# Retention part of a two-layer decoder trunk: state products first, a PSUM bank for each head, squares summed by ScalarE's accumulator

## The chip, the cores and the metric

The kernel runs on one core of a Trainium2 chip. The metric is the device time of one execution in microseconds (us). The core's engines are named as in the profile: PE (TensorE matmuls), PEld (its weight loads), DVE (VectorE), ACT (ScalarE), POOL (GpSimd) and SP (SyncE, which here only issues loads).

## What is computed

Two layers over 512 tokens of width 1024. Each layer normalises x, projects it, runs three mixers side by side (retention, stick-breaking attention, a state-space model), gates them, projects and adds. The change lies in retention alone:

```
def retention(q, k, v, q_norm, k_norm, out_norm, cos, sin):
    ...
    inner = jnp.einsum('bnhij,bnjhe->bnihe', scores, vc)        # within a chunk of 128 tokens
    ...
    def step(state, kv):
        return state * chunk_decay + kv, state
    _, prev = lax.scan(step, jnp.zeros_like(chunk_kv[0]), chunk_kv)
    cross = jnp.einsum('bnihd,nbhde->bnihe', qc * q_decay[:, :, None], prev)
    out = (inner + cross).reshape(B_, S_, RET_HEADS, RET_V_DIM)
    out = rmsnorm(out, out_norm.reshape(RET_HEADS, RET_V_DIM))  # per head, over 256 columns
```

There are 4 heads with 128 columns of q and k and 256 of v, and 4 chunks of 128 tokens.

## The kernel before, in words

**Main work and slots.** The body of a layer is a list of pieces of projection (`mains`), each 12 or 24 matmuls of 128x512 into a tile `mm`, at one piece for each slot. A full-precision product is made of three fp32r ones (`three`): weight and activation are split into a high and a low part. ScalarE makes the high part of a weight tile (`wh`), VectorE the low one (`wl`); SP loads the raw tile. All else is written as generators: `spawn(gen, slot)` puts one in a slot, `yield n` moves its rest n slots on, and `yield 0` puts its rest behind the matmuls of the same slot (`late`). The order of instructions on each engine is the order in which this program writes them; nothing is reordered afterwards. An engine that waits holds back everything behind it in its own queue.

**Buffers.** PSUM has 8 banks: three for `mm`, five for everything else (`psm`, pool `ps_sm`, a bank for each tile). SBUF work tiles (`bt`) come from one pool of 48. A new tile takes a buffer that an earlier tile gives back, and its first writer waits for the last reader of that one.

**Retention.** `ret_chunk(n)` runs for chunk n = 0..3, three slots apart, when q, k and v of all chunks are there. It makes the scores of 4 heads in one tile `rs` (four fp32 products of 128x128), masks them into `sT`, and then goes through two parts c = 0, 1 of two heads each; below, part (n, c) is part c of chunk n. Between parts lie two slots, so that the parts of neighbouring chunks interleave: (0,0), (0,1), (1,0), (1,1), (2,0), (2,1), (3,0), (3,1). A part splits v (`rvsh`, `rvsl`), scores (`sTs`) and k (`kts`) and has on PE

- the output tile `ro`, 128x512, one bank: for each of its two heads three split products of 128x256 and, for n > 0, one fp32 product of the chunk's q with the running state (two PE instructions in the trace, `ro<-state,rT`);
- for n < 3 the update of the state, `rkv`, one bank, six split products.

After the matmuls of the slot the state is copied (n = 0, L1252) or added up on DVE from `rkv`, ScalarE squares `ro` into `sq2` (L1258), DVE sums the squares of each head (TENSOR_REDUCE, L1260), and POOL makes the factor `rs` = (mean + eps)^-0.5. Two slots later (`K["t3"]`) DVE writes `yt` = `ro` times the factor; this is the last reader of the bank. Later, `rz_evac` transposes `yt` on PE into `yaT`.

Of the five small banks a part holds one for `ro` over these two slots, and one for `rkv` until the state is updated; the next chunk's `rs` holds one until `sT` is made.

Of the kernel before, what the change touches and what calls it, by code (L numbers as in the profile page):

```python
# [13 lines left out]
AF = mybir.ActivationFunctionType  # L14
ALU = mybir.AluOpType
PSUM = bass.MemoryType.PSUM

P = 128
# [168 lines left out]
def trunk(ctx: ExitStack, tc, x_in, w_in, par_in, bc_in, ng_in, cst_in, rope_in, out):  # L187
    nc = tc.nc
    load = {"V": 0.0, "G": 0.0, "T": 0.0}

    def counted(f, engine, each):


        def g(*a, **k):
            o = k["out"] if "out" in k else a[0]
            load[engine] += 0.07 * (engine != "T") + each * math.prod(o.shape[1:])
            return f(*a, **k)  # L197

        return g

    TT = counted(nc.vector.tensor_tensor, "V", 1.04e-3)
    TS = counted(nc.vector.tensor_scalar, "V", 1.04e-3)
    STT = counted(nc.vector.scalar_tensor_tensor, "V", 1.2e-3)
    GT, GS = counted(nc.gpsimd.tensor_tensor, "G", 2.2e-3), counted(nc.gpsimd.tensor_scalar, "G", 1.2e-3)
    ACT = nc.scalar.activation
    MM = counted(nc.tensor.matmul, "T", 0.42e-3)
# [9 lines left out]
    def bt(name, dt=F32, shape=(P, 512)):  # L216
        return bp.tile(list(shape), dt, tag="b", name=name)

    def st(name, n):
        return sp.tile([P, n], F32, tag="s", name=name, padded_shape=[P, 64])  # L220
# [4 lines left out]
    def psm(name):  # L225
        return ps_sm.tile([P, 512], F32, tag="sm", name=name)
# [14 lines left out]
    def C(n):  # L241
        o, s = CST[n]
        return cst[:, o : o + s]
# [7 lines left out]
        out=negm, in_=negm, pattern=[[1, P]], base=0, channel_multiplier=-1, compare_op=ALU.is_ge, fill=0.0  # L251
# [25 lines left out]
    def rsqrt_mean(out_, ssum, n, eps, cols):  # L277

        t = st("ms", cols)
        GS(out=t, in0=ssum, scalar1=1.0 / n, scalar2=eps, op0=ALU.mult, op1=ALU.add)  # L280
        GT(out=out_, in0=t, in1=mhalf[:, :cols], op=ALU.pow)

    def split(src, name, shape=(P, 512)):
        h = bt(name + "h", F32R, shape)
        l = bt(name + "l", F32R, shape)
        ACT(h, src, AF.Copy)
        TT(out=l, in0=src, in1=h.bitcast(F32), op=ALU.subtract)
        return h, l

    def packed(src, name, op=TT):  # L290
        t = bt(name, F32R)
        ACT(t[:, 0:256], src, AF.Copy)
        op(out=t[:, 256:512], in0=src, in1=t[:, 0:256].bitcast(F32), op=ALU.subtract)
        return t
# [45 lines left out]
    def three(ps, a, b, first, last):  # L340

        MM(ps, a[0], b[0], start=first, stop=False)
        MM(ps, a[0], b[1], start=False, stop=False)
        MM(ps, a[1], b[0], start=False, stop=last)
# [321 lines left out]
    def v3(ap, n=32):  # L666
        return ap.rearrange("p (g m) -> p g m", m=n)
# [173 lines left out]
    def layer(l, last, base):  # L841
# [311 lines left out]
        qT, kT, ktok = [], [], [None] * NT  # L1153
        rv = [[None] * 2 for _ in range(NT)]
        ytok = [[None] * 2 for _ in range(NT)]
# [50 lines left out]
        state = [None, None]  # L1206

        def ret_chunk(n):
            pt = psm("rs")
            for h in range(4):  # L1210
                hs = slice(h * P, h * P + P)
                MM(pt[:, hs], kT[n][:, hs], qT[n][:, hs], start=True, stop=True)
            yield 0
            sT = bt("sT")
            TT(out=v3(sT, P), in0=v3(pt, P), in1=C("tri").unsqueeze(1).to_broadcast(r4h), op=ALU.mult)
            keep = n < NT - 1

            def halves(c):

                cs = slice(256 * c, 256 * c + 256)  # L1220
                return (
                    split(rv[n][c], "rvs"), packed(sT[:, cs], "sTs"),
                    packed(ktok[n][:, cs], "kts", GT) if keep else None,
                )

            part = halves(0)
            yield K["t1"]
            for c in range(2):
                vs, sTs, ks = part
                po = psm("ro")  # L1230
                for i in range(2):
                    h = 2 * c + i
                    hs = slice(h * P, h * P + P)
                    sl = slice(256 * i, 256 * i + 256)
                    two = [slice(P * i, P * i + P), slice(256 + P * i, 256 + P * i + P)]
                    v = [x[:, sl] for x in vs]
                    three(po[:, sl], [sTs[:, x] for x in two], v, True, n == 0)
                    if n:
                        MM(po[:, sl], qT[n][:, hs], state[c][:, sl], start=False, stop=True)
                if keep:  # L1240
                    pk = psm("rkv")
                    for i in range(2):
                        h = 2 * c + i
                        sl = slice(256 * i, 256 * i + 256)
                        two = [slice(P * i, P * i + P), slice(256 + P * i, 256 + P * i + P)]
                        three(pk[:, sl], [ks[:, x] for x in two], [x[:, sl] for x in vs], True, True)
                yield 0
                if not keep:
                    pass
                elif n == 0:  # L1250
                    state[c] = bt(f"state{c}")
                    nc.vector.tensor_copy(out=state[c], in_=pk)  # L1252
                else:
                    TT(out=state[c], in0=state[c], in1=pk, op=ALU.add)
                if c == 0:
                    part = halves(1)
                s2 = bt("sq2")
                ACT(s2, po, AF.Square)  # L1258
                ss, rs = st("ss", 2), st("rs", 2)
                nc.vector.tensor_reduce(out=ss, in_=v3(s2, 256), axis=mybir.AxisListType.X, op=ALU.add)  # L1260
                rsqrt_mean(rs, ss, 256, EPS, 2)
                yield K["t3"]
                ytok[n][c] = bt("yt")
                TT(out=v3(ytok[n][c], 256), in0=v3(po, 256), in1=rs.unsqueeze(2).to_broadcast([P, 2, 256]), op=ALU.mult)

        def rz_evac(m, ps):
            pt = psm("yaT")
# [93 lines left out]
        for n in range(NT):  # L1361
            spawn(ret_chunk(n), at["rv1"] + K["ret0"] + K["ret_gap"] * n)
# [14 lines left out]
        for name, m in mains:  # L1377
            i = now[0]
# [22 lines left out]
    while due:  # L1401
        i = min(due)
# [28 lines left out]
```

## Time and profile before

| | |
|---|---|
| device time, median of 3 runs (range) | 1289.89 us (1289.74 to 1291.02) |
| device time of the profiled execution | 1291.43 us |
| its span, first to last instruction | 1289.7 us |
| PE busy | 1271.6 us, 99% |
| PEld, DVE, ACT, POOL busy | 1051.8, 845.1, 536.9, 388.4 us |
| mean granted TensorE clock | 0.996 of full speed |

PE is the engine that is hardly ever idle, so a change shows in the time where it makes PE wait or takes work or a wait from it. The 1.73 us between time and span lie outside the profiled instructions. The time of the profiled execution is 1.54 us above the median.

### The profile page before, as it was taken

How to read it: one execution, taken by the hardware profiler on the slowest of the kernel's cores; microseconds unless marked ns; L12 is line 12 of the kernel's file. 1: busy time of each engine (PE TensorE's matmuls, PEld its weight loads, DVE VectorE, ACT ScalarE, POOL GpSimd, SP SyncE). 2: the span in 40 equal slices, each digit the busy share in tenths (PEclk: the TensorE clock that was granted, in tenths of full speed). 3: DMA queues.
4: the chain of work that ended last, by engine and by line, in shares of the span. 5: the costliest groups of instructions: out<-in, count | busy, mean ns of one | idle time of the engine just before them, and what ended most of it. 6: DMA issues, size and time to landing. Idle time of an engine off the chain costs nothing.

```text
span 1289.7 us, 16710 instructions
## 1 busy us (share of the span) xinstructions
PE 1271.6 (99%) x6388; PEld 1051.8 (82%) x6388; DVE 845.1 (66%) x1192; ACT 536.9 (42%) x919; POOL 388.4 (30%) x453
## 2 busy tenths in 40 slices
PE   8999999999999999999999989999999999999998
PEld 6887788888888888888888877888888888888887
DVE  6988976866784448555374678778657834675542
ACT  5444454454444433332343545534534544433311
POOL 3314743546531012000052136444565311210000
PEclk9999999999999999999999989999999999999999
DMA  5323222124223322234442312122231232222342
GB/s 211 101 96 98 67 66 82 66 82 131 66 66 99 98 75 72 84 97 155 147 166 72 98 49 66 49 83 82 96 101 66 70 127 82 66 82 83 97 137 75
DMA packets 37235, 119.53 MB, mean 93 GB/s; under 512 B 4130, under 2 KB 4770, under 8 KB 37156
## 3 DMA queue, kind: packets, MB, share of 16 engines
q1 hardware_dynamic: 29376, 104.87, 25.1%
q10 hardware_dynamic: 7780, 13.60, 3.1%
q8 instruction: 50, 0.82, 0.3%
q14 instruction: 29, 0.24, 0.1%
HBM read 114.26 MB, written 4.19 MB: 92 GB/s over the span
## 4 chain that ended last, share of the span: by engine, by line
PE 82%; DVE 3%; ACT 1%; issue 0%; DVEq 0%; ACTq 0%
PE mm L197 71%; PE T L411 2%; PE ro L197 2%; PE py L197 1%; DVE kp L1083 1%; PE S L197 1%; PE sbo L197 1%; PE wt L1100 1%; DVE w L197 1%; PE z L197 1%; PE rkv L197 1%; PE rs L197 1%; PE yaT L1269 1%; DVE ks L197 0%; DVE ybl L197 0%; PE pk L197 0%
## 5 line engine op out<-in xcount | busy, mean ns | idle before, releaser
L197 DVE TENSOR_TENSOR wl<-raw,wh 128x1024 fp32r<-128x1024 f32 x196 | 249.6, 1280 | 100.8 <-ACT wh L320 97.1
L197 PE MATMUL mm<-hh,wh 128*128 128x512 f32 x640 | 256.2, 400 | 0.0
L197 PE MATMUL mm<-hh,wl 128*128 128x512 f32 x640 | 250.8, 392 | 0.0
L197 PE MATMUL mm<-hl,wh 128*128 128x512 f32 x640 | 250.8, 392 | 0.0
L320 ACT ACTIVATE wh<-raw 128x1024 fp32r<-128x1024 f32 x196 | 206.3, 1058 | 61.8 <-PE mm L197 24.7
L197 PE MATMUL mm<-wh,hh 128*128 128x512 f32 x512 | 206.7, 404 | 0.4 <-ACT hh L434 0.4
L197 PE MATMUL mm<-wl,hh 128*128 128x512 f32 x512 | 201.8, 394 | 0.3 <-DVE wl L197 0.3
L197 PE MATMUL mm<-wh,hl 128*128 128x512 f32 x512 | 201.7, 394 | 0.0
L197 PEld LDWEIGHTS mm<-hh,wh 128*128 128x128 f32 x640 | 121.2, 189 | 25.6 <-issue 1.8
L197 PEld LDWEIGHTS mm<-hh,wl 128*128 128x128 f32 x640 | 120.7, 189 | 26.1
L197 PEld LDWEIGHTS mm<-hl,wh 128*128 128x128 f32 x640 | 121.0, 189 | 23.5
L197 PEld LDWEIGHTS mm<-wl,hh 128*128 128x128 f32 x512 | 104.8, 205 | 18.6 <-DVE wl L197 2.0
L197 PEld LDWEIGHTS mm<-wh,hl 128*128 128x128 f32 x512 | 104.5, 204 | 18.2 <-DVE hl L197 0.3
L197 PEld LDWEIGHTS mm<-wh,hh 128*128 128x128 f32 x512 | 104.6, 204 | 17.9 <-ACT hh L434 0.8
L1026 ACT ACTIVATE gate<-mm 128x512 f32<-128x512 f32 x48 | 28.6, 596 | 118.2 <-PE mm L197 118.2
L1083 DVE TENSOR_TENSOR_SCAN kp<-kp,zero 128x511 f32<-128x511 f32 (+1 forms) x64 | 60.3, 962 | 22.8 <-ACT kp L1079 22.7
L197 POOL TENSOR_SCALAR ms<-ss 128x8 f32<-128x8 f32 (+3 forms) x56 | 19.1, 341 | 181.9 <-DVE ss L855 101.0
L197 POOL TENSOR_TENSOR rs<-ms,mhalf 128x8 f32<-128x8 f32 (+3 forms) x56 | 64.7, 1155 | 4.7
L853 ACT ACTIVATE sq<-mm 128x512 f32<-128x512 f32 x32 | 19.0, 592 | 85.8 <-PE mm L197 85.7
L197 PE MATMUL mm<-wl,mgh 128*128 128x512 f32 (+1 forms) x136 | 51.5, 378 | 0.2
L197 PE MATMUL mm<-wh,mgh 128*128 128x512 f32 (+1 forms) x136 | 51.3, 377 | 0.0
L197 PE MATMUL mm<-wh,mgl 128*128 128x512 f32 (+1 forms) x136 | 51.3, 377 | 0.0
(258 smaller groups left out, 2244.5 us busy)
## 6 DMA issues: line engine op xcount, KB each, us to landing
raw<-in_w SPq DMA_DIRECT2D x196, 512.0 KB, 3.6
x<-in_x SPq DMA_DIRECT2D x8, 256.0 KB, 7.1
rope<-in_rope ACTq DMA_DIRECT2D x8, 256.0 KB, 4.1
xh<-in_x ACTq DMA_DIRECT2D x8, 256.0 KB, 4.8
x<-xh ACTq DMA_DIRECT2D x8, 256.0 KB, 2.0
xh<-x ACTq DMA_DIRECT2D x8, 256.0 KB, 4.5
out<-xh ACTq DMA_DIRECT2D x7, 256.0 KB, 2.0
br<-in_bc ACTq DMA_DIRECT2D x2, 256.0 KB, 2.9
```

The source lines that it names most:

```text
L197: return f(*a, **k)
L320: ACT(wh, raw, AF.Copy)
L411: nc.tensor.transpose(pt[:, i * P : i * P + P], src[:, i * P : i * P + P], ident)
L853: ACT(s2, ps, AF.Square)
L1026: ACT(sg, ps, AF.Sigmoid)
L1083: nc.vector.tensor_tensor_scan(v, v, zero1.to_broadcast([P, n - 1]), 1.0, ALU.mult, ALU.add)
L1100: nc.tensor.transpose(pt[:, i * P : i * P + P], wblk(h, b, kb), ident)
L1269: nc.tensor.transpose(pt[:, t * P : t * P + P], ytok[t][m // 4][:, (m % 4) * P : (m % 4) * P + P], ident)
```

## The change

For each part, `ro` becomes two tiles, one for each head, each with a bank of its own and 256 of its 512 columns in use. For n > 0 the two state products stand first, then the six split products. ScalarE squares each head's half with its accumulator, which leaves the sum of squares in `ss`, so the TENSOR_REDUCE on DVE goes; and `yt` is written by two TENSOR_SCALAR instructions of 256 columns, one for each head, instead of one TENSOR_TENSOR of 512.

```
-                po = psm("ro")
+                po = [psm("ro")[:, 0:256] for i in range(2)]
+
+                for i in range(2 if n else 0):
+                    hs = slice((2 * c + i) * P, (2 * c + i) * P + P)
+                    MM(po[i], qT[n][:, hs], state[c][:, 256 * i : 256 * i + 256], start=True, stop=False)
                 for i in range(2):
-                    h = 2 * c + i
-                    hs = slice(h * P, h * P + P)
                     sl = slice(256 * i, 256 * i + 256)
                     two = [slice(P * i, P * i + P), slice(256 + P * i, 256 + P * i + P)]
-                    v = [x[:, sl] for x in vs]
-                    three(po[:, sl], [sTs[:, x] for x in two], v, True, n == 0)
-                    if n:
-                        MM(po[:, sl], qT[n][:, hs], state[c][:, sl], start=False, stop=True)
+                    three(po[i], [sTs[:, x] for x in two], [x[:, sl] for x in vs], n == 0, True)
...
                 s2 = bt("sq2")
-                ACT(s2, po, AF.Square)
                 ss, rs = st("ss", 2), st("rs", 2)
-                nc.vector.tensor_reduce(out=ss, in_=v3(s2, 256), axis=mybir.AxisListType.X, op=ALU.add)
+                for i in range(2):
+                    ACT(s2[:, 256 * i : 256 * i + 256], po[i], AF.Square, accum_out=ss[:, i : i + 1])
                 rsqrt_mean(rs, ss, 256, EPS, 2)
                 yield K["t3"]
                 ytok[n][c] = bt("yt")
-                TT(out=v3(ytok[n][c], 256), in0=v3(po, 256), in1=rs.unsqueeze(2).to_broadcast([P, 2, 256]), op=ALU.mult)
+                for i in range(2):
+                    TS(out=ytok[n][c][:, 256 * i : 256 * i + 256], in0=po[i], scalar1=rs[:, i : i + 1], scalar2=None, op0=ALU.mult)
```

What it does to the order, at three places. In these rows a tile has its number, and `[waits X]` names the engines whose work the row waits for beyond what its engine has already seen done.

PE in part (1,0) of the first layer, before: `ro_4386` is its output tile, `state0_4249` the state of the first two heads, `rkv_4395` its state update.

```order
L197 MATMUL ro_4386<-rvsh_4309,sTs_4313 128x256 [waits Activation_49]
L197 MATMUL ro_4386<-rvsl_4310,sTs_4313 128x256 [waits DVE_49]
L197 MATMUL ro_4386<-rvsh_4309,sTs_4313 128x256 [waits DVE_49]
L197 MATMUL ro_4386<-state0_4249,rT_3673 128x256
L197 MATMUL ro_4386<-rvsh_4309,sTs_4313 128x256
L197 MATMUL ro_4386<-rvsl_4310,sTs_4313 128x256
L197 MATMUL ro_4386<-rvsh_4309,sTs_4313 128x256
L197 MATMUL ro_4386<-state0_4249,rT_3673 128x256
L197 MATMUL rkv_4395<-rvsh_4309,kts_4316 128x256 [waits PE_49,Activation_49]
```

The same place now; `ro_4389` and `ro_4390` are the banks of its two heads.

```order
L197 MATMUL ro_4389<-state0_4250,rT_3673 128x256 [waits DVE_49]
L197 MATMUL ro_4390<-state0_4250,rT_3673 128x256 [waits DVE_49]
L197 MATMUL ro_4389<-rvsh_4310,sTs_4314 128x256 [waits Activation_49]
L197 MATMUL ro_4389<-rvsl_4311,sTs_4314 128x256
L197 MATMUL ro_4389<-rvsh_4310,sTs_4314 128x256
L197 MATMUL ro_4390<-rvsh_4310,sTs_4314 128x256
L197 MATMUL ro_4390<-rvsl_4311,sTs_4314 128x256
L197 MATMUL ro_4390<-rvsh_4310,sTs_4314 128x256
L197 MATMUL rkv_4399<-rvsh_4310,kts_4317 128x256 [waits DVE_49,Activation_49]
```

The state products moved to the front, the last split product is now the last of the group, and `rkv`, which waited for PE and ACT, now waits for DVE: its bank is that of the state update of part (0,1), `rkv_4339`, whose reader is the COPY of the state (`state1_4371`) on DVE.

PE in part (1,1), before, up to its state update:

```order
L197 MATMUL ro_4496<-rvsh_4428,sTs_4432 128x256 [waits Activation_49]
L197 MATMUL ro_4496<-rvsl_4429,sTs_4432 128x256 [waits DVE_49]
L197 MATMUL ro_4496<-rvsh_4428,sTs_4432 128x256 [waits DVE_49]
L197 MATMUL ro_4496<-state1_4368,rT_3673 128x256
...
L197 MATMUL rkv_4505<-rvsh_4428,kts_4435 128x256 [waits PE_49,Activation_49]
```

The same place now:

```order
L197 MATMUL ro_4502<-state1_4371,rT_3673 128x256 [waits DVE_49]
L197 MATMUL ro_4503<-state1_4371,rT_3673 128x256 [waits DVE_49]
L197 MATMUL ro_4502<-rvsh_4432,sTs_4436 128x256 [waits Activation_49]
L197 MATMUL ro_4502<-rvsl_4433,sTs_4436 128x256
...
L197 MATMUL rkv_4512<-rvsh_4432,kts_4439 128x256 [waits DVE_49,Activation_49]
```

The first two products now wait for DVE, each for one of the two `yt` instructions of part (0,1): the two banks are those of `ro_4331` and `ro_4332`, the outputs of that part. `rkv_4512` has the bank of the scores `rs_4458` and waits for their reader, `sT_4479`.

DVE between parts (1,0) and (2,0), as it stands now. `yt_4463` belongs to part (0,1) and is what the rows just shown wait for; `yt_4499` belongs to part (1,0), and the products of part (2,0) wait for it in the same way.

```order
L197 TENSOR_TENSOR wl_4451<-raw_4206,wh_4450 128x1024 [waits DMAHW4_49,Activation_49]
L197 TENSOR_SCALAR yt_4463<-ro_4331,rs_4375 128x256 [waits Pool_49]
L197 TENSOR_SCALAR yt_4463<-ro_4332,rs_4375 128x256
L197 TENSOR_TENSOR sT_4479<-rs_4458,cst_77 128x512 [waits PE_49]
L197 TENSOR_TENSOR rvsl_4482<-rv_3772,rvsh_4481 128x512 [waits PE_49,Activation_49]
L197 TENSOR_TENSOR sTs_4485<-sT_4479,sTs_4485 128x256 [waits Activation_49]
L197 TENSOR_TENSOR wl_4492<-raw_4274,wh_4491 128x1024 [waits DMAHW5_49,Activation_49]
L197 TENSOR_TENSOR gate_2701<-mm_4466,gate_2701 128x512
L197 TENSOR_TENSOR gate_1165<-gate_1165,gate_2701 128x512 [waits DVE_49]
L197 TENSOR_SCALAR yt_4499<-ro_4389,rs_4444 128x256 [waits Pool_49]
L197 TENSOR_SCALAR yt_4499<-ro_4390,rs_4444 128x256
L197 TENSOR_TENSOR state1_4371<-state1_4371,rkv_4512 128x512
```

Each `yt` is two rows where it was one, and a row `TENSOR_REDUCE ss<-sq2` is gone ahead of the first row and again behind the last; the rest has kept its place. The same holds for the second layer, whose tiles have other numbers and the same waits.

## Rows read from the trace of the kernel before

**Rows 1.** Busy time in a stretch: PE, PEld, DVE, ACT, POOL, clock, DMA.

```profile
440.00:560.00 120.00, 120.00 (x598) 101.44 (x598) 71.68 (x97) 43.64 (x68) 15.71 (x21) 1.00 0.26 80
```

**Rows 2.** Timeline of PE, first layer: start, duration, engine, line, instruction, tiles.

```profile
465.19 0.28 PE L197 MATMUL ro<-rvsh,sTs 128*128 128x256 f32 x1
465.30 0.28 PE L197 MATMUL ro<-rvsl,sTs 128*128 128x256 f32 x1
...
466.21 0.28 PE L197 MATMUL ro<-rvsh,sTs 128*128 128x256 f32 x1
...
466.57 0.47 PE L197 MATMUL rkv<-rvsh,kts 128*128 128x256 f32 x1
...
476.56 0.28 PE L197 MATMUL ro<-rvsh,sTs 128*128 128x256 f32 x1
...
477.94 0.47 PE L197 MATMUL rkv<-rvsh,kts 128*128 128x256 f32 x1
...
481.59 0.28 PE L197 MATMUL ro<-rvsh,sTs 128*128 128x256 f32 x1
...
490.24 0.28 PE L197 MATMUL ro<-rvsh,sTs 128*128 128x256 f32 x1
```

**Rows 3.** Timeline of DVE in the same stretch; the last row is of the second layer.

```profile
466.53 0.69 DVE L1252 COPY state<-rkv 128x512 f32<-128x512 f32 x1 [3.19 <-PE ro L197]
...
475.33 1.23 DVE L197 TENSOR_TENSOR wl<-raw,wh 128x1024 fp32r<-128x1024 f32 x1 [0.26 <-ACT wh L320]
476.48 0.68 DVE L197 TENSOR_TENSOR yt<-ro,rs 128x512 f32<-128x512 f32 x1
477.90 0.69 DVE L197 TENSOR_TENSOR sT<-rs,cst 128x512 f32<-128x512 f32 x1 [0.74 <-PE ro L197]
...
480.76 1.23 DVE L197 TENSOR_TENSOR wl<-raw,wh 128x1024 fp32r<-128x1024 f32 x1 [0.73 <-ACT wh L320]
...
483.23 0.68 DVE L197 TENSOR_TENSOR yt<-ro,rs 128x512 f32<-128x512 f32 x1
...
490.93 0.68 DVE L197 TENSOR_TENSOR yt<-ro,rs 128x512 f32<-128x512 f32 x1
...
1122.26 0.68 DVE L197 TENSOR_TENSOR yt<-ro,rs 128x512 f32<-128x512 f32 x1
```

**Rows 4.** Timeline of ACT in the same stretch.

```profile
467.55 0.60 ACT L1258 ACTIVATE sq<-ro 128x512 f32<-128x512 f32 x1 [5.59 <-PE rkv L197]
...
473.75 0.60 ACT L1258 ACTIVATE sq<-ro 128x512 f32<-128x512 f32 x1 [0.84 <-POOL kts L197]
474.25 1.05 ACT L320 ACTIVATE wh<-raw 128x1024 fp32r<-128x1024 f32 x1
...
479.04 0.42 ACT L292 ACTIVATE sTs<-sT 128x256 fp32r<-128x256 f32 x1
```

**Rows 5.** Timeline of ACT between the layers, where it already sums by accumulator.

```profile
642.78 0.63 ACT L417 ACTIVATE xn<-xh 128x512 f32<-128x512 f32 x1 [4.72 <-DVE xh L197]
643.32 0.19 ACT L417 ACTIVATION_READ_ACCUMULATOR xn<-xh 128x1 f32 x1
643.41 1.06 ACT L434 ACTIVATE hh<-T 128x512 fp32r<-128x512 f32 x2
```

**Rows 6.** Groups by form: tiles, shapes, count | busy, mean ns | idle before.

```profile
L1079 ACT ACTIVATE kp<-z 128x256 f32<-128x256 f32 x16 | 6.2, 390 | 0.0
...
L197 DVE TENSOR_SCALAR kk<-pk,cst 128x256 f32<-128x256 f32 x8 | 3.9, 482 | 0.6 <-PE pk L197 0.6
```

**Rows 7.** Busy time and clock around PE's two longest pairs of waits.

```profile
143.20:145.74 2.54, 0.30 (x1) 0.14 (x1) 2.33 (x5) 1.14 (x3) 0.00 (x0) 0.94 0.60 206
145.60:148.60 3.00, 2.86 (x12) 2.67 (x13) 2.90 (x4) 1.24 (x3) 1.61 (x1) 0.50 0.00 0
746.75:750.49 3.74, 0.30 (x1) 0.14 (x1) 3.53 (x5) 1.12 (x3) 2.78 (x2) 0.88 0.50 140
749.70:756.30 6.60, 5.81 (x18) 4.95 (x19) 6.30 (x7) 1.92 (x3) 2.95 (x3) 0.50 0.00 0
```

## The prediction

> **What bounds the kernel now.** I read the busy times and the list of waits first: PE is busy 1271.6 of 1289.7 us, and its 18.1 us of idle time lie outside retention. The table of a stretch over the retention shows PE busy 120.00 of 120.00 us at full clock, with DVE busy 71.68 and ACT 43.64 [rows 1]. So nothing that DVE or ACT saves there can be won by PE, which runs at the end of every wait; the change pays only where it adds work or a wait to PE. I then went through PE's timeline around the three parts after the first two, and through those of DVE and ACT beside it, to see when the buffers that the new order needs come free [rows 2 to 4].
>
> **PE's own work** stays: as many products of the same shapes. In part (1,0) the group begins at 465.19 with a pitch of 0.11 to 0.12; the state update's first record at 466.57 lasts 0.47 where a split product lasts 0.28, so it was 0.19 queued behind the fp32 state product and really started at 466.76 [rows 2]. The eight products take 1.57 us, in either order. Six split products at 0.12 leave (1.57 - 0.71)/2 = 0.43 for a state product. One change less between the two kinds of product in a group has no row of its own; it could be worth at most that queueing, 0.19 for each of 12 groups, 2.3 us in all; I take 0, since the pitch goes on through both kinds.
>
> **DVE and ACT.** Gone are 16 reduces over 512 columns, each taken like a yt of 512: a record of 0.68, of which 0.08 overlaps (yt starts at 476.48, the wl before it ends at 476.56 [rows 3]), so 16 x 0.60 = 9.6 us. The 16 yt become 32 instructions; the nearest one, 128x256 by a factor per partition, takes 0.48 [rows 6], 0.40 to the next by the same overlap, so a yt takes 0.80 for 0.60: +3.2 us. DVE saves 6.4 us. On ACT a square of 512 holds the engine 0.50 (473.75 to the wh at 474.25 [rows 4]). Two of 256 take 0.27 each, by rows of 0.39 [rows 6] less an overlap of 0.12 (0.60 less 0.50 in the row just read gives 0.10), and each accumulator adds 0.13: after one, the next instruction starts 0.63 after its square where 0.50 is the plain interval [rows 5]. That is 0.80 for 0.50, +0.3 for each of 16 parts, 4.8 us.
>
> The Trainium skill ("Perfetto Trace Analysis", Optimizing Scalar/DVE Operations) gives an overhead per instruction on PSUM of about 125 ns for DVE and 51 ns for ScalarE, and advises larger operations. It speaks against both splits; as an estimate from it alone the squares cost 0.05 more each, not 0.3, and the sum below would be 8.1 us in place of 9.1.
>
> **The banks** are the dear part. A chunk now takes seven small banks for five (two outputs a part), and there are still five. Which tile inherits which bank follows from the order of allocation; I followed it on PE from (1,0) on.
>
> *State update of (1,0).* Its bank was that of the state update of (0,1), whose reader is DVE's COPY. The COPY is itself late: its buffer is read last by the products of (1,0), behind whose last split product it starts 0.04 us later (466.21 + 0.28 = 466.49, COPY at 466.53) [rows 2, 3]. That split product is now the last of the group: start 466.76 - 0.12 = 466.64, end 466.92, COPY 466.96 to 467.65. With 0.1 from DVE's end to PE's start (an estimate; PE to DVE is the 0.04) the update starts at 467.75 in place of 466.76: **+1.0**. Bounds 0.8 (the COPY's length and a little) and 1.0.
>
> *Output of (1,1).* PE comes at 476.56 + 1.0 = 477.56 [rows 2] and needs the two banks of (0,1), which the yt of (0,1) gives back. That yt stood at 476.48 [rows 3], when the single bank it held was not yet wanted. Its chain: the square of (0,1) at 467.55 starts behind the state update of (1,0) [rows 4], so +1.0; its two accumulators make everything behind it +1.3, the split of v and scores, POOL's kts, and the square of (1,0) at 473.75, which waited for kts; that one's accumulators make wh at 474.25 and wl at 475.33 [rows 3, 4] +1.6. The reduce that was before that wl doesn't help, since wl waits for wh (0.26 idle in its row). So yt starts at 476.48 + 1.6 = 478.08, its first half ends at 478.56, its second at 478.96; PE starts at 478.66, **+1.1**. The second half is ready while the first state product (0.43) runs. Bounds: 0.75 (the squares cost 0.05 and the hand-over nothing) and 1.7 (the accumulator's read of 0.19 [rows 5] comes twice on top of it).
>
> *State update of (1,1).* Its bank is that of the scores, whose reader sT waits for the second state product, as it waited for the last one before (sT at 477.90, 0.74 idle [rows 3]). That product ends at 478.66 + 2 x 0.43 + 0.16 = 479.68, sT runs 479.72 to 480.41, the update starts at 480.5 where the products would allow 480.23: **+0.27**. Bounds 0 and 0.4.
>
> *Output of (2,0).* PE came at 481.59, and the banks are those of (1,0), given back by a yt that stood at 483.23, behind a wl at 480.76 and two gates [rows 2, 3]. That chain begins with ScalarE's sTs at 479.04 [rows 4], behind the state update of (1,1), so it and PE are both shifted by 2.37. The first half ends at 483.23 + 0.48 = 483.71, and 0.1 later PE may go: 483.81 - 481.59 = **+2.2**. Bounds 2.0 and 2.3.
>
> *From (2,1) on.* PE comes there at 490.24 + 4.6 = 494.8, the yt of (1,1) was at 490.93 [rows 2, 3] and is half done 0.6 to 2 us before that even if it shifts by 2.7; the later parts have no state update or more room. I take 0; the cover is this half microsecond at least, and if it were gone, (2,1) would wait about as (1,1) does, +1.1.
>
> The sum is 1.0 + 1.1 + 0.27 + 2.2 = 4.55 a layer. The second layer has the same rows 639.03 us later (yt at 1122.26 for 483.23 [rows 3]) and the same waits: **9.1 us**, bounds 7.8 and 10.2.
>
> **PE's clock.** After PE had been idle for 2.24 of 2.54 us the granted clock was 0.50, the 1.2 GHz level, for 3.0 us; after 3.44 idle of 3.74 us it was 0.50 for 6.6 us [rows 7]. At half clock half of that is lost: 1.5 and 3.3 us. The 2.2 us before (2,0) is as long as the first of these, so I add 1.5 a layer, 3.0 in all; bounds 0 and 6.6. The 1 us waits have no such row here and get nothing.
>
> **The rivals.**
> - *The waits, and the clock stays full.* PE is idle for less than in the row of 143 us, or has been dense for longer ahead of it. Then +9.1, 1299.0 us. Against it: the lengths are almost alike.
> - *A long fall*, as at 749.7 us, in both layers: +9.1 + 6.6, 1305.6 us. For it: 1.1 and 0.27 of idle time lie shortly ahead of the 2.2. Against it: that row has 3.4 us.
> - *The state update of (1,0) isn't held*, because the COPY is released earlier than by the last split product. Then 3.6 a layer, 1297.1 us with the clock full. Against it: the 3.19 idle that PE's ro ended ahead of the COPY [rows 3].
> - *The other side: no wait at all.* DVE, 6.4 us lighter, brings each yt ahead of PE, and the two banks turn in time: 1289.9 us, or a little less where the order of products saves its 0.19. It decides from the point where the yt of (0,1) comes 1.1 us and that of (1,0) 2.2 us earlier than worked out. For it: DVE has idle time throughout. Against it: just this idle time; the yt follows a wl that waits for ScalarE, which gets slower. The Trainium skill ("Perfetto Trace Analysis", Matmuls) says that independent groups should rotate through PSUM banks so that the evacuation of one overlaps the products of the next; if a bank for each head did that here, this would be the outcome.
>
> **How the numbers follow.** Chances: the forecast 0.58, full clock 0.22, long fall 0.06, update not held 0.08, no wait 0.06. The profiled execution's 1291.43 would become 1291.43 + 9.1 + 3.0 = 1303.5; it lies 1.54 above the median, so against the median 1289.89 + 12.1 = **1302.0 us**. The likeliest case alone spans 1289.89 + 7.8 + 1.5 = 1299.2 (the clock falls in one layer) to 1289.89 + 10.2 + 3.0 = 1303.1. The range goes from the third rival at its lower bounds (0.75 + 2.0 + 0.05 = 2.8 a layer, 1295.5) to the long fall at the upper ones (10.2 + 6.6, 1306.7). A measurement of this kernel can tell about 0.2%, 2.6 us, from no change: faster 0.02, same 0.04 (the last rival), slower 0.94.
>
> **What the changed profile would show.** PE's list of waits gains ro behind DVE yt four times (two near 1.1, two near 2.2), rkv behind the COPY of the state twice (1.0, perhaps recorded as 0.8), rkv behind sT twice (0.3); none at (2,1), (3,0), (3,1). PE's idle time goes from 18.1 to about 27, and two stretches of some 3 us at clock 0.50 stand behind the output of (2,0), near 486 and 1130 us. DVE has 16 reduces less and is some 6 us less busy, ACT has 32 reads of accumulators more and is some 5 us busier. I'd be wrong if no yt ends a wait of PE, if the COPY starts before the last split product of its part ends, or if the state-first order itself changes the length of a group by more than 0.2 us.

## The result and the profile after

The changed kernel takes 1304.19 us (median of 5 runs, 1301.40 to 1304.25), the one before 1289.89 us (1289.19 to 1291.02): a ratio of 1.0095 with a 95% interval of 1.0084 to 1.0106. It is slower. (The two medians by themselves give 1.0111, 14.3 us; the ratio means 12.3 us. How the ratio is formed from the runs is not on record; 12.1 us were forecast.) The time lies 2.2 us above the forecast of 1302.0, within its range, but 1.1 above the 1303.1 at which the prediction ended its likeliest case. The profiled execution took 1304.19 us, with a span of 1302.5 us, 12.8 more than before.

The page, part 1, of the changed kernel: PE is busy 5.4 us longer and idle 25.5 us where it was idle 18.1; DVE has 4.9 us less, ACT 3.9 us more and 48 instructions more.

```profile
PE 1277.0 (98%) x6388; PEld 1055.1 (81%) x6388; DVE 840.2 (65%) x1192; ACT 540.8 (42%) x967; POOL 383.1 (29%) x453
```

The list of what PE waited for, in total, with the number of times and the longest:

```profile
PE wt L1100 <- DVE w L197: 10.2, 9, 2.1
PE ro L197 <- DVE yt L197: 5.5, 4, 2.0
PE gain L452 <- POOL negm L249: 2.3, 1, 2.3
PE rkv L197 <- DVE state L1251: 1.8, 2, 0.9
PE T L411 <- DVE xn L197: 0.9, 1, 0.9
PE mm L197 <- ACT hh L434: 0.6, 1, 0.6
PE rkv L197 <- DVE sT L197: 0.3, 2, 0.2
```

The second, fourth and last rows are new: eight waits, four in each layer, 7.6 us as recorded. Each stands at one place in the timeline of PE (start, duration, and in brackets the wait ahead of it and what ended it). The first five rows are the output of (1,0), its state update, the output of (1,1), its state update, and the output of (2,0); the last three are of (2,1), of the second layer's part (2,0), and of its split products:

```profile
465.42 1.02 PE L197 MATMUL ro<-state,rT 128*128 128x256 f32 x4
...
468.02 0.36 PE L197 MATMUL rkv<-rvsh,kts 128*128 128x256 f32 x1 [0.88 <-DVE state L1251]
...
478.83 1.13 PE L197 MATMUL ro<-state,rT 128*128 128x256 f32 x4 [0.77 <-DVE yt L197]
...
480.84 0.36 PE L197 MATMUL rkv<-rvsh,kts 128*128 128x256 f32 x1 [0.17 <-DVE sT L197]
...
486.54 1.58 PE L197 MATMUL ro<-state,rT 128*128 128x256 f32 x4 [2.00 <-DVE yt L197]
...
496.87 1.02 PE L197 MATMUL ro<-state,rT 128*128 128x256 f32 x4
...
1131.72 1.63 PE L197 MATMUL ro<-state,rT 128*128 128x256 f32 x4 [2.01 <-DVE yt L197]
1132.79 0.78 PE L197 MATMUL ro<-rvsh,sTs 128*128 128x256 f32 x1
```

They answer to [rows 2]. Part (1,0) starts at 465.42 where it started at 465.19, so 0.23 has to be taken off before a row is compared. DVE in the same stretch, which answers to [rows 3]:

```profile
467.18 0.69 DVE L1251 COPY state<-rkv 128x512 f32<-128x512 f32 x1 [3.43 <-PE ro L197]
...
477.16 1.23 DVE L197 TENSOR_TENSOR wl<-raw,wh 128x1024 fp32r<-128x1024 f32 x1 [3.12 <-ACT wh L320]
478.30 0.87 DVE L197 TENSOR_SCALAR yt<-ro,rs 128x256 f32<-128x256 f32 x2
480.00 0.69 DVE L197 TENSOR_TENSOR sT<-rs,cst 128x512 f32<-128x512 f32 x1 [0.83 <-PE ro L197]
...
484.68 0.68 DVE L197 TENSOR_TENSOR gate<-mm,gate 128x512 f32<-128x512 f32 x1
485.40 0.69 DVE L197 TENSOR_TENSOR gate<-gate 128x512 f32<-128x512 f32 x1
486.01 0.87 DVE L197 TENSOR_SCALAR yt<-ro,rs 128x256 f32<-128x256 f32 x2
486.79 0.68 DVE L197 TENSOR_TENSOR state<-state,rkv 128x512 f32<-128x512 f32 x1
```

These rows show who holds PE: the COPY ends at 467.87 and the state update starts at 468.02; the yt from 478.30 on gives the output of (1,1) its banks, and sT, which ends at 480.69, the update at 480.84; the yt at 486.01 stands behind two gates while PE waits for it. And ScalarE, which answers to [rows 4]:

```profile
475.33 0.39 ACT L1259 ACTIVATE sq<-ro 128x256 f32<-128x256 f32 x1 [0.84 <-POOL kts L197]
475.62 0.19 ACT L1259 ACTIVATION_READ_ACCUMULATOR sq<-ro 128x1 f32 x1
475.71 0.38 ACT L1259 ACTIVATE sq<-ro 128x256 f32<-128x256 f32 x1
475.97 0.20 ACT L1259 ACTIVATION_READ_ACCUMULATOR sq<-ro 128x1 f32 x1
476.06 1.06 ACT L320 ACTIVATE wh<-raw 128x1024 fp32r<-128x1024 f32 x1
```

From the first square to wh it takes 0.73 where one square of 512 took 0.50. The windows behind the output of (2,0) in the first and the second layer, read as in [rows 1] (the clock is the third number from the end):

```profile
486.50:490.50 4.00, 3.96 (x17) 3.69 (x18) 2.27 (x4) 1.09 (x5) 0.89 (x2) 0.57 0.20 80
1131.70:1135.70 4.00, 3.98 (x17) 3.71 (x18) 2.24 (x4) 1.07 (x4) 0.89 (x2) 0.57 0.18 75
```

TensorE ran at 1.2 GHz there for most of 4 us, in both layers; the split product of 1132.79 lasts 0.78 for it.

### The profile page after: what moved, and what is told of

Read it like the earlier page. It is cut to its first block, busy times and chain, and to the rows that moved or that the text cites. A ratio compares the mean times of both kernels' runs of the same rounds, so it can differ in the third digit from the quotient of the medians.

```text
span 1302.5 us, 16747 instructions
## 1 busy us (share of the span) xinstructions
PE 1277.0 (98%) x6388; PEld 1055.1 (81%) x6388; DVE 840.2 (65%) x1192; ACT 540.8 (42%) x967; POOL 383.1 (29%) x453
## 4 chain that ended last, share of the span: by engine, by line
PE 79%; DVE 5%; ACT 2%; issue 0%; POOL 0%; DVEq 0%; ACTq 0%
PE mm L197 68%; PE T L411 2%; PE ro L197 2%; PE py L197 1%; PE wt L1100 1%; DVE kp L1083 1%; PE S L197 1%; PE sbo L197 1%; PE rkv L197 1%; DVE wl L197 1%; PE z L197 1%; DVE w L197 1%; ACT wh L320 1%; PE yaT L1269 1%; DVE gate L197 0%; PE rs L197 0%
## 5 line engine op out<-in xcount | busy, mean ns | idle before, releaser
L197 DVE TENSOR_TENSOR wl<-raw,wh 128x1024 fp32r<-128x1024 f32 x196 | 250.8, 1286 | 114.5 <-ACT wh L320 110.8
L197 POOL TENSOR_SCALAR ms<-ss 128x8 f32<-128x8 f32 (+3 forms) x56 | 15.7, 281 | 180.8 <-DVE ss L855 101.5
L197 POOL TENSOR_TENSOR rs<-ms,mhalf 128x8 f32<-128x8 f32 (+3 forms) x56 | 61.0, 1088 | 4.7
L197 DVE TENSOR_TENSOR gate<-mm,gate 128x512 f32<-128x512 f32 x48 | 33.0, 688 | 29.4 <-PE mm L197 29.4
```

## The experiments

They are compared by the measured ratio and, since one execution varies by a microsecond or two in stretches that the change doesn't touch, by a number that leaves those out: the time from the last transpose `T<-ident,m` ahead of retention to the first `yaT` behind it, on PE. Before it is 106.53 us in the first layer (405.57 to 512.10) and 106.52 in the second (1044.61 to 1151.13); after, 112.88 and 112.90, so 6.35 and 6.38 us more. The kernel before was run again beside the experiments, with medians of 1291.16 us, and 1290.93 beside the last two. The ratios are against these; the times expected start from 1289.89, and so from some 1.1 to 1.3 us less.

**One bank, all else of the change.** The edit against the changed kernel; each head's state product now stands ahead of its own three split products:

```
-                po = [psm("ro")[:, 0:256] for i in range(2)]
+                po = psm("ro")
...
+                    if n:
+                        MM(po[:, sl], qT[n][:, hs], state[c][:, sl], start=True, stop=False)
+                    three(po[:, sl], [sTs[:, x] for x in two], v, n == 0, True)
```

> Everything of the change except the second bank: output of a part in one bank again, each head's state product ahead of its three split products, squares with accumulators, yt in two halves. Theory (the loss is the bank's): no wait of PE for ro or rkv is left, no stretch at half clock in retention, 1289.9 us within 1 us. Rival 1 (the accumulators lengthen ScalarE's chain and PE waits for it whatever the bank): some of the 14.3 us stays, 1292 to 1300. Rival 2 (the state-first order is itself longer or shorter for PE): up to 0.19 for each of 12 groups, 1287.6 to 1292.2.

Measured: median 1290.56 us, ratio 0.9996 (0.9987 to 1.0005), span 1288.9, stretches 106.50 and 106.50 us. PE's whole list of waits:

```profile
PE wt L1100 <- DVE w L197: 10.4, 10, 2.1
PE gain L452 <- POOL negm L249: 2.2, 1, 2.2
PE T L411 <- DVE xn L197: 1.2, 1, 1.2
PE mm L197 <- DVE wl L197: 0.4, 1, 0.4
```

No wait of retention is in it. Accumulators, yt in halves and the state product ahead of its split products cost nothing and win nothing as long as the bank stays one; DVE was busy 838.6 us, 6.5 us less than before, and PE took none of it. (Both state products ahead of all six split products were not run with one bank; in the changed kernel that order leaves the group of (1,0) at 1.57 us, 465.42 to 466.99, as before.)

**Two banks, nothing else.** The edit against the kernel before; the squares are in halves, and so is yt (two TENSOR_SCALAR, not shown here), since each bank holds a half:

```
-                po = psm("ro")
+                po = [psm("ro")[:, 0:256] for i in range(2)]
...
-                ACT(s2, po, AF.Square)
+                for i in range(2):
+                    ACT(s2[:, 256 * i : 256 * i + 256], po[i], AF.Square)
```

> Only the second bank: product order of before, squares without accumulators (two of 256), the reduce on DVE as before, yt in two halves. Theory: the same four waits a layer. State update of (1,0): the COPY starts at its old time, so 0.6 instead of 1.0; output of (1,1): no accumulators and 0.4 less shift, about 0.5; state update of (1,1): sT now waits for the last state product at the end of its group, about 0.6; output of (2,0): 2.2. Sum 3.9, with 1.6 for the clock 5.5 a layer, 1301 us (range 1299 to 1303). Rival 1 or 2 (accumulators or order are the cause): 1290 to 1292.

Measured: median 1301.27 us, ratio 1.0077 (1.0065 to 1.0090), span 1299.6, stretches 112.55 and 112.54 us. The new rows in PE's list, and their four places in the first layer:

```profile
PE ro L197 <- DVE yt L197: 5.2, 4, 2.1
...
PE rkv L197 <- DVE state L1252: 0.9, 2, 0.4
PE rkv L197 <- DVE sT L197: 0.9, 2, 0.4
```

```profile
465.44 0.36 PE L197 MATMUL rkv<-rvsh,kts 128*128 128x256 f32 x1 [0.45 <-DVE state L1252]
...
475.98 0.36 PE L197 MATMUL ro<-rvsh,sTs 128*128 128x256 f32 x1 [0.49 <-DVE yt L197]
...
478.23 0.36 PE L197 MATMUL rkv<-rvsh,kts 128*128 128x256 f32 x1 [0.44 <-DVE sT L197]
...
484.02 0.36 PE L197 MATMUL ro<-rvsh,sTs 128*128 128x256 f32 x1 [2.10 <-DVE yt L197]
```

The same four places wait, for the same tiles, in the sizes expected (0.6, 0.5, 0.6 and 2.2 with the 0.1 to 0.2 that a record leaves out); only the sum expected was somewhat short, 5.5 for the 6.0 us that each stretch grew by (112.55 - 106.53). So the bank alone is 6.0 of the 6.35 us of the first layer.

**The yt first in its slot.**

```
+                def ahead(gen):
+                    yield 0
+                    then(gen)
+
+                spawn(ahead(scale_out()), now[0] + K["t3"] - 1)
                 yield K["t3"]
-                ytok[n][c] = bt("yt")
...
```

(`scale_out` is the generator that allocates yt and writes its halves.)

> The whole change, but each yt is issued at the start of its slot, so that the two gates (0.6 to 0.7 each) that stood ahead of the yt of (1,0) come behind it. Theory: the wait before (2,0) falls from 2.0 to about 0.7 as recorded, the others stay, 3.4 us a layer; a gap that short leaves the clock at its full level, so 1289.9 + 6.8 = 1296.7 (1296 to 1298). Rival (the clock falls because of all the waits of the stretch together): the 1.6 a layer stays, 1299.5 to 1300.5. Rival (the wait is of something other than the gates' place in DVE's queue): nothing moves, 1304.

Measured: median 1299.89 us, ratio 1.0067 (1.0055 to 1.0080), span 1297.9, stretches 110.78 and 110.79 us. PE and, below, the clock behind the output of (2,0) in either layer:

```profile
483.60 1.13 PE L197 MATMUL ro<-state,rT 128*128 128x256 f32 x4 [0.69 <-DVE yt L197]
...
486.00 0.36 PE L197 MATMUL rkv<-rvsh,kts 128*128 128x256 f32 x1 [0.57 <-DVE state L197]
```

```profile
483.60:487.60 4.00, 3.43 (x20) 2.98 (x21) 3.93 (x7) 2.09 (x8) 1.11 (x2) 1.00 0.40 131
1127.80:1131.80 4.00, 3.35 (x20) 2.90 (x21) 3.93 (x8) 2.00 (x8) 1.03 (x2) 1.00 0.42 131
```

The wait fell from 2.00 to 0.69 as worked out, and the clock stayed at 2.4 GHz in both layers, against the rival of the summed waits. But the time came out higher than the 1296 to 1298 expected, and within the range of that rival, which the time alone would have borne out. I had missed a fifth wait: the update of (2,0) takes the bank of the update of (1,1), whose reader is the state's sum on DVE, behind yt and gates. In the changed kernel the 2.0 us ahead of it had covered it. So the stretch is 4.25 us above before (110.78 - 106.53), not 3.4.

**The yt ahead of the weights.** The same, but yt is issued at the end of the slot before:

```
+                def scale_out(n=n, c=c, po=po, rs=rs):
+                    yield 0
+                    ytok[n][c] = bt("yt")
...
+                spawn(scale_out(), now[0] + K["t3"] - 1)
                 yield K["t3"]
```

> The whole change, but each yt is issued at the end of the slot before its own, ahead of the low part of the weights (wl 1.23) and the gates. Theory: both waits of ro for yt go, and the clock with them; the waits for the COPY (0.9 as recorded, 1.0) and for sT (0.2, 0.4) stay: 1.4 a layer, 1292.8 us (1292 to 1294). Rival (the banks are only part of it, PE waits for ScalarE's longer chain): the waits change their name to rvsh or sTs and 1296 or more stays. A new wait is possible: wl comes 0.8 later, and the matmuls that read it may wait, up to 0.8 at each of 8 parts.

Measured: median 1295.73 us (1292 to 1294 expected), ratio 1.0038 (1.0026 to 1.0051), span 1292.9, stretches 108.94 and 108.97 us.

```profile
PE rkv L197 <- DVE state L1251: 1.7, 2, 0.9
PE rkv L197 <- DVE state L197: 1.5, 2, 0.7
...
PE rkv L197 <- DVE sT L197: 0.3, 2, 0.2
```

Both waits of ro are gone, PE doesn't wait for ScalarE in their place, and of what is left (2.4 us a stretch) 1.4 were expected; the rest is the fifth wait again (0.74 as recorded at 483.85). Moving wl back by a yt added no wait of its own: `mm` waited for `wl` 0.2 us in the whole execution.

**In addition, a buffer of its own for the state.**

```
+            if n == 0:
+                state[1] = bt("state1")
+                nc.gpsimd.memset(state[1], 0.0)
             yield K["t1"]
...
-                    state[c] = bt(f"state{c}")
+                    if c == 0:
+                        state[c] = bt(f"state{c}")
```

> As yt_before_weights (each yt ahead of the weights' low part), and the state of the second two heads is written once by GpSimd early in chunk 0 (a memset), so that it has a buffer of its own and its COPY no longer takes over that of sTs of (1,0). Theory: the COPY runs before the products of (1,0), the update of (1,0) waits no more: the 0.87 as recorded, 1.0 really, goes in each layer, and the span falls from 1292.9 to 1290.9; what is left are the waits for sT (0.17) and for the state's sum before the update of (2,0) (0.74). Rival (the update of (1,0) waits for the bank whatever the COPY's buffer is): its wait stays near 0.9 and the span near 1292.9.

Measured: median 1294.05 us, ratio 1.0024 (1.0015 to 1.0033), span 1291.3 (1290.9 expected), stretches 107.86 and 107.86 us, 1.1 less than without it.

```profile
PE rkv L197 <- DVE state L197: 1.5, 2, 0.8
...
PE rkv L197 <- DVE sT L197: 0.3, 2, 0.2
```

The wait for the COPY is gone: it had come from the COPY's own buffer, not from the bank alone. With three of the five waits taken out, 1.3 us a stretch are left of 6.35. It doesn't beat the kernel before, and there is nothing in these runs by which two banks could: with one bank PE waits for nothing here.

**The change without accumulators.**

```
-                    ACT(s2[:, 256 * i : 256 * i + 256], po[i], AF.Square, accum_out=ss[:, i : i + 1])
+                    ACT(s2[:, 256 * i : 256 * i + 256], po[i], AF.Square)
+                nc.vector.tensor_reduce(out=ss, in_=v3(s2, 256), axis=mybir.AxisListType.X, op=ALU.add)
```

> The whole change, but the two squares without accumulators and the reduce on DVE again. Theory (two accumulated squares cost ScalarE 0.3 more, and two such pairs stand ahead of the yt that the output of (1,1) waits for): that wait falls by 0.5, from 0.77 to about 0.25 as recorded; the waits for the COPY (0.88), for sT (0.17) and before (2,0) (2.0, with the clock's fall) stay; span 1302.5 - 1.1 = 1301.4. Rival (the accumulators are off PE's path, as their idle engine suggests): the wait stays 0.77 and the span 1302.5. Rival (the reduces on DVE are on the path and cost more than the accumulators): the wait grows, span above 1302.5.

Measured: median 1302.56 us, ratio 1.0093 (1.0079 to 1.0106), span 1299.7, stretches 110.95 and 112.53 us. The output of (1,1) and of (2,0) in the first layer, then of (2,0) in the second:

```profile
477.73 1.13 PE L197 MATMUL ro<-state,rT 128*128 128x256 f32 x4 [0.41 <-DVE yt L197]
...
485.43 1.13 PE L197 MATMUL ro<-state,rT 128*128 128x256 f32 x4 [2.00 <-DVE yt L197]
486.21 0.47 PE L197 MATMUL ro<-rvsh,sTs 128*128 128x256 f32 x1
...
1128.98 2.02 PE L197 MATMUL ro<-state,rT 128*128 128x256 f32 x4 [2.01 <-DVE yt L197]
1130.44 0.78 PE L197 MATMUL ro<-rvsh,sTs 128*128 128x256 f32 x1
```

The wait at (1,1) fell from 0.77 to 0.41, so the accumulators are on the path there, for 0.36 us a layer instead of the 0.5 expected, and the reduces, back on DVE, are not (the wl behind them, at 476.05, still waits 0.26 us for wh). The second layer's 112.53 is 0.37 below 112.90, the same again. In the first layer this execution shows something else: after the same wait of 2.00 us the clock stayed full.

```profile
485.40:489.40 4.00, 3.97 (x23) 3.57 (x24) 3.96 (x7) 2.40 (x7) 1.58 (x3) 1.00 0.18 74
1128.90:1132.90 4.00, 3.92 (x16) 3.57 (x17) 2.90 (x6) 0.95 (x3) 0.89 (x2) 0.57 0.19 78
```

The two stretches of one execution, alike but for that, differ by 112.53 - 110.95 = 1.58 us: this is what the fall costs. It also accounts for most of the span's being 2.8 below that of the changed kernel where 1.1 was expected; the ratios, 1.0093 and 1.0095, can't tell the two kernels apart.

## Why the prediction was right

**The mechanism held.** Each wait came at the place, for the tile and in the order foretold, none came at (2,1) or later, and the two undoing runs show the cause: one bank with all the rest, no loss; two banks with nothing else, 6.0 of 6.35 us.

**The sum, term by term** (first layer, 0.23 taken off). State update of (1,0): 468.02 where 466.99 would have been due, 1.03 for a predicted 1.0. Output of (1,1): PE is there at 476.56 + 0.23 + 1.03 = 477.82 and starts at 478.83, 1.01 for 1.1. State update of (1,1): 478.83 + 1.57 = 480.40, starts at 480.84, 0.44 for 0.27. Output of (2,0): 481.59 + 0.23 + 2.48 = 484.30, starts at 486.54, 2.24 for 2.2. Together 4.72 for 4.57 (the prediction adds its four terms up to 4.55, a slip). What the stretch has beyond that, 6.35 - 4.72 = 1.63, I put down to the clock, for 1.5; the run without accumulators measured 1.58 for it. The two layers make 12.7 of the span's 12.8. So of the 2.2 us above the forecast the terms account for some 0.65; the other 1.54 is that the forecast started from a median of before that lay that much below its profiled execution, while the changed kernel's profiled execution is its median.

**Luck in the second term.** The yt of (0,1) came 1.59 late (478.30 - 476.48 - 0.23), for a predicted 1.6, but by two errors against each other: two pairs of accumulated squares added 0.46, not 0.6, and the first square of the chain, at 468.89 on ScalarE, started 1.11 late, not 1.0. The bounds were worked out with less care than the terms. Their ends add up to 3.55 and 5.4 a layer, 7.1 and 10.8 in all, where the prediction has 7.8 and 10.2; and by its own condition (both squares at 0.05, no hand-over) the lower bound of the output of (1,1) is 0.5, not 0.75. The measured time lies far from these ends.

**The step that was mis-sized most** is the state update of (1,1). Its hand-over from DVE to PE is 0.15 (480.69 to 480.84, and 467.87 to 468.02 at the COPY), where I had taken 0.1, and the two state products ahead of sT take 1.13 when the second bank comes free only after the first (1.02 at (2,1), where nothing is waited for). The hand-over is not one number: at the two outputs it is 0.05 (the first half of the yt at 486.01 ends 0.48 later, at 486.49, and PE starts at 486.54).

**The accumulators** cost ScalarE 0.73 - 0.50 = 0.23 a part, not 0.3: 3.9 us in all (540.8 - 536.9) for a predicted 4.8. On PE's path they cost 0.36 a layer. The estimate of 0.05 more for a pair of squares, which the prediction worked out from the Trainium skill ("Perfetto Trace Analysis", Optimizing Scalar/DVE Operations), fits the two plain squares better than the accumulated ones: 0.55 from the first of them to wh (474.41 to 474.96) in the run without accumulators. The reads of the accumulators (0.19 to 0.20 each, half of it hidden) are what it leaves out. The same section of the Trainium skill advises larger operations if the engine is saturated, a condition that the prediction left out; ScalarE, busy 42%, is not.

**DVE** had 4.9 us less, for 6.4. The run with one bank, which has the same DVE instructions, had 6.5 less, and the two halves of yt take 0.87 as expected (0.48 + 0.40), so the estimate of the edits holds. The yt take 13.9 us in both runs, so the 1.6 us between them lie in work that the edits don't touch: wl took 250.8 and 249.5 us, the `sTs` 7.9 and 6.8, and groups of the state-space model differ both ways. PE wins nothing by either.

**The clock** fell in both layers, as in the likeliest case, and cost 1.6 each time. But the condition given for it was too simple: a wait of 2.0 us was followed by 1.2 GHz in five of the six places profiled (both layers of the changed kernel and of the two banks alone, one of the run without accumulators) and by full clock in the sixth; waits of 0.7, with yt first in its slot, were followed by full clock in both layers. The rival "the clock stays full" is thus something that single layers of single executions do. It is not special to retention either. PE's pair of waits near 144 us, from which the prediction took its term, is 1.51 and 0.74 us in all eight profiled executions; the clock fell behind it in three (before, after, and the run without accumulators) and stayed full in five. Two of them, with the state's own buffer and without accumulators:

```profile
140.00:150.00 10.00, 7.75 (x39) 6.16 (x38) 9.66 (x11) 5.37 (x10) 6.24 (x6) 1.00 0.19 52
...
140.00:150.00 10.00, 7.75 (x33) 6.06 (x32) 9.66 (x11) 4.89 (x9) 6.28 (x6) 0.83 0.17 52
```

So the trace of before showed one of two outcomes of that wait, and that the clock fell in both layers of the profiled execution was in part luck. The lowest of the five times, 1301.40 us, is 2.8 us below the median, and its mean granted clock was 0.995 where the profiled execution has 0.993; one or two falls less, in retention or elsewhere, could explain it, but that run has no trace here. What decides between the two outcomes stays open.

**The rival on the other side** failed at the point named for it: the yt came 1.0 and 2.2 us too late, because they follow a wl that waits for ScalarE (the second stands behind two gates as well), and a lighter DVE only has more idle time ahead of that (3.12 ahead of the wl at 477.16). The rule of the Trainium skill that stood behind it ("Perfetto Trace Analysis", Matmuls: rotate independent groups through PSUM banks) did not pay here: the two halves are evacuated one right behind the other, two slots after their products, and with two banks a part each group of eight products comes round to a used bank sooner.

**What I didn't foresee** is the wait behind the wait: the update of (2,0) would itself have had to wait 0.6 to 0.7 us for the state's sum. It costs nothing in the changed kernel and appears as soon as the wait ahead of it is shortened.

## What to carry to other kernels

Where PE never waits, count buffers and not busy time: a change that takes seven banks a round where five are to be had made PE wait here for the readers of earlier tiles, and relief on an engine with idle time bought nothing. Follow for each new tile whose buffer it inherits, where that reader stands in its engine's queue, and what that queue waits for; the sum of such waits came out within 0.2 us of 4.7 a layer here. When one wait is mended, look for the next one that it had covered, before writing down the gain.

## What the runs showed that was not expected

- The same wait of 2.0 us was followed by half the clock in one layer and by full clock in the other layer of one execution, 1.58 us apart; behind a pair of waits that is alike in all eight kernels, near 144 us, the clock fell in three executions and not in five.
- A COPY can be late for its destination: the state's SBUF buffer had been that of scores still being read, and a memset that gave it another one took 1.1 us off each layer.
